# An encoder step on one core: projections emitted tile by tile, with the first norm, the gates, the mixer's first tiles and the tail put in another order

## The chip, the core and the metric
The kernel runs on one core of a Trainium2 chip. The core has a matrix engine (TensorE, in the profile PE, with its weight loads as PEld), a vector engine (VectorE, DVE), a scalar engine (ScalarE, ACT), GpSimd (POOL), and DMA queues, most of them issued by SyncE (SP). Each engine works through its own list of instructions in order and waits for the others on semaphores. The metric is the device time of one execution in microseconds; three timed executions are given by their median.

## What is computed
One layer of a streaming encoder for 576 positions: 512 of a new stream, 64 of a running one with 1024 cached positions. `T` is 576, `D` is 1024; the arrays stand transposed, features on the 128 partitions and positions along a row.

```python
h = rmsnorm(x, g_attn);  z = h @ w_in
q, k, v, f_lin, q_c, c_kv, k_r = split(z)        # 3 x 512 | 8 | 384 | 256 | 32
logf = log_sigmoid(f_lin + b_f)                  # the gates; F = cumsum(logf)
fox = softmax(q k^T / 8 + F[t] - F[s], causal) v              # 8 heads x 64
q_full = rmsnorm(q_c, g_q) @ w_q_up;  c_kv = rmsnorm(c_kv, g_kv)   # the latent norms
mla = softmax((q_lat c_kv^T + rope(q) rope(k_r)^T) / sqrt(96), chunk mask) c_kv w_uv   # 8 heads
x = x + concat(fox, mla) @ w_out
u = rmsnorm(x, g_ffn) @ w_up                      # 2 x 2816 columns
x = x + (silu(conv(gate)) * conv(value)) @ w_down
y = rmsnorm(x, final_norm)
```

Keys, values, gates, latents and the last rows of `u` are outputs as well.

## The kernel before
Every product of full precision is three matmuls: weights and inputs are split into a high and a low part, and low x high, high x high and high x low are added up in PSUM. A weight block of 128x1024 is loaded as `wr`, ScalarE writes its high part and VectorE or GpSimd its low part into `wh` (both have two buffers). PSUM has eight banks in rings: `g` two, `s` three, `t` two, `o` one. A projection tile (`in_tile`) is 48 matmuls over two `g` banks, one bank for each half of the 576 positions; VectorE evacuates them, scaled by `R`, the reciprocal root of the first norm.

The stages, with the times of the profiled execution: to about 20 us `x` is loaded and split and the first key tile, the gates' logits and the rope key are computed beside it; the first norm follows (`sq_sum`, `col_sums`, `rstd`), whose squares ScalarE makes, whose adds go to GpSimd and VectorE by the string `acc0`, and whose sum over partitions is a matmul with `ones`. Projections and attention over 16 heads fill the time to 320 us: FoX in pairs of heads (`fox_gemm(p)`: key, query and value tile of pair p), then MLA. W_out takes until 369 us, the mixer until 784 us, the tail until the end: the last down projection in two halves of the positions (320, then 256), each with the final norm and its output (`L994` on GpSimd, `L996` on VectorE).

What sets the order: five generators (projections, scores and values of the heads, and the same for the running stream) are interleaved by a planner that goes by the costs they yield. The lists thus emitted are then arranged, engine by engine, by a list scheduler of the framework. The projections' generator is `s_gemm`. Its sequence is pair 0 (ahead of it), then pair 1, the five latent tiles `l0` to `l4` (`latent`), pair 2, the two latent norms (`latent_norm`, with their matmuls by `ones`), pair 3, then the keys and queries of MLA, of which the query up-projection is the first to read the normalised and split latents (`xs`). `gates()` is called after all three tiles of pair 1; its result `cf` holds the decay factors that the running stream's scores (L523) read. The mixer (`up_conv`, `gemm`) takes tile after tile; its input is the split and scaled `x2` (`split_scaled`, L267), which is complete only when W_out is.

Of the kernel before, what the change touches and what calls it, by code (L numbers as in the profile page):

```python
# [11 lines left out]
AF = mybir.ActivationFunctionType  # L12
# [43 lines left out]
    "sq0": "a", "acc0": "gggvvv", "sq": "agv", "acc": "gvvv",  # L56
# [9 lines left out]
TPOOL = (0, 1)  # L66

W0 = 6
# [3 lines left out]
def build(nc, tc, io):  # L72
# [177 lines left out]
    def rstd_of(v, y, a, out):  # L250
        S.activation(y, v, AF.Ln)
        S.activation(y, y, AF.Exp, scale=-0.5)
        newton(v, y, a, out)

    def newton(v, y, a, out):
        V.tensor_tensor(a, y, y, op=ALU.mult)
        V.scalar_tensor_tensor(a, a, -0.5, v, op0=ALU.mult, op1=ALU.mult)
        V.scalar_tensor_tensor(out, a, 1.5, y, op0=ALU.add, op1=ALU.mult)

    def rstd(ps, n, out):  # L260
        v, y, a = (raw()[:, :T] for _ in range(3))
        evac(lambda d, p, c: V.tensor_scalar(d, p, 1.0 / n, EPS, op0=ALU.mult, op1=ALU.add), v, ps)
        rstd_of(v, y, a, out)
# [183 lines left out]
    def fox_gemm(p):  # L447
        ps = k0 if p == 0 else in_tile(p)
        k = raw()
        evac(lambda d, p, c: V.tensor_tensor(d, p, R[:, c], op=ALU.mult), k, ps)  # L450
        G.dma_start(io["o_k"][p], k[:, :T])
        ps = in_tile(4 + p)
        q = raw()
        evac(lambda d, p, c: V.scalar_tensor_tensor(d, p, FOX_SCALE, R[:, c], op0=ALU.mult, op1=ALU.mult), q, ps)
        ps = in_tile(8 + p)
# [3 lines left out]
        return q, k, v  # L459
# [96 lines left out]
    fx = {0: fox_gemm(0)}  # L556
    gate = {}

    def gates():
        S.activation(z, z, AF.Identity, bias=bf)  # L560
        mn = raw()[:8, :T]
        V.scalar_tensor_tensor(mn, z, -1.0, z, op0=ALU.mult, op1=ALU.min)
        e = raw()[:8, :T]
        S.activation(e, mn, AF.Exp)
        up = raw()[:8, :T]
# [5 lines left out]
        logf = raw()[:8, :T]  # L571
# [4 lines left out]
        fp = raw()[:8, :T]  # L576
# [166 lines left out]
    def s_gemm():  # L743
        for p in range(1, 4):
            if p >= 2:
                yield ("after", ("stack", 2 * (p - 2) + 1), 0)
            fx[p] = fox_gemm(p)
            if p == 1:
                gates()
            yield ("done", 23.1, ("up", p))  # L750
            if p == 1:
                for a in range(5):
                    latent(a)
                    if a == 2:
                        rope_key()
                    if a == 1:
                        acc_c = sq_sum(craw)
                    if a == 4:
                        acc_q = sq_sum(qcr)
# [143 lines left out]
    def g_tile():  # L903
# [9 lines left out]
        return t[0][:, k * 1152:(k + 1) * 1152].rearrange("p (a b) -> p a b", a=2)  # L913

# [44 lines left out]
    for hf, (o, w) in enumerate(HC):  # L959
# [138 lines left out]
```

## Time and profile before

| | |
|---|---|
| median of three timed executions | 809.66 us (807.43 to 810.17) |
| the profiled execution | 810.69 us, of which the span 808.9 |
| TensorE busy | 772.8 us (96%), 5582 matmuls |
| VectorE, ScalarE, GpSimd busy | 508.5, 340.6, 264.0 us |
| mean granted clock of TensorE | 0.988 of 2.4 GHz |

A granted clock of 1.00 is 2.4 GHz, 0.50 is 1.2 GHz; the clock has these two levels, and a value between them is a mean over a stretch that holds both. Matmuls overlap, so a busy TensorE is not one at its peak; a stretch in which it is idle is one in which it waits.

### The profile page before, as it was taken

How to read it: one execution, taken by the hardware profiler on the slowest of the kernel's cores; microseconds unless marked ns; L12 is line 12 of the kernel's file. 1: busy time of each engine (PE TensorE's matmuls, PEld its weight loads, DVE VectorE, ACT ScalarE, POOL GpSimd, SP SyncE). 2: the span in 40 equal slices, each digit the busy share in tenths (PEclk: the TensorE clock that was granted, in tenths of full speed). 3: DMA queues.
4: the chain of work that ended last, by engine and by line, in shares of the span. 5: the costliest groups of instructions: out<-in, count | busy, mean ns of one | idle time of the engine just before them, and what ended most of it. 6: DMA issues, size and time to landing. Idle time of an engine off the chain costs nothing.

```text
span 808.9 us, 14256 instructions
## 1 busy us (share of the span) xinstructions
PE 772.8 (96%) x5582; PEld 743.3 (92%) x5582; DVE 508.5 (63%) x941; ACT 340.6 (42%) x611; POOL 264.0 (33%) x390
## 2 busy tenths in 40 slices
PE   8898999999899989999999999999999999999994
PEld 8796899897789879999999999999999999999993
DVE  6838554878677763457867524676425667675356
ACT  7224652457667864124443212343113433433231
POOL 5134342336143230223333221433222343332034
PEclk9998999999999999999999999999999999999997
DMA  9373423545563741222222223222232222222313
GB/s 329 111 212 109 109 84 106 145 107 169 129 152 80 185 131 30 80 79 79 72 85 68 79 92 105 79 79 60 79 98 80 103 80 79 79 66 83 105 40 117
DMA packets 33811, 83.98 MB, mean 104 GB/s; under 512 B 6006, under 2 KB 9350, under 8 KB 33744
## 3 DMA queue, kind: packets, MB, share of 16 engines
q1 hardware_dynamic: 31520, 78.55, 32.6%
q0 software_dynamic: 1008, 3.19, 1.1%
q10 hardware_dynamic: 1216, 1.33, 0.5%
q8 instruction: 44, 0.72, 0.4%
q14 instruction: 23, 0.19, 0.1%
HBM read 64.12 MB, written 5.49 MB: 86 GB/s over the span
## 4 chain that ended last, share of the span: by engine, by line
PE 76%; DVE 10%; ACT 5%; DMA 3%; issue 3%; SPq 1%; POOL 1%; DVEq 0%; ACTq 0%; POOLq 0%
PE g L210 31%; PE s L210 19%; PE t L210 12%; PE g L438 3%; PE g L969 1%; DMA mix<-xT 1%; DVE B L382 1%; DVE xs L267 1%; PE s L720 1%; PE t L375 1%; ACT p L326 1%; PE s L969 1%; DMA A<-qr 1%; PE s L522 1%; DVE raw L135 1%
## 5 line engine op out<-in xcount | busy, mean ns | idle before, releaser
L210 PE MATMUL g<-xs,wh 128*128 128x288 f32 (+2 forms) x2028 | 281.1, 295 | 0.3 <-ACT spt L128 0.2
L210 PEld LDWEIGHTS g<-xs,wh 128*128 128x128 f32 x2028 | 271.1, 189 | 1.7 <-ACT spt L128 0.4
L194 ACT ACTIVATE wh<-wr 128x1024 fp32r<-128x1024 f32 (+4 forms) x106 | 99.8, 942 | 204.3 <-PE g L210 88.4
L135 POOL TENSOR_TENSOR wh<-wr,wh 128x1024 fp32r<-128x1024 f32 (+3 forms) x51 | 111.8, 2192 | 216.5 <-ACT wh L194 173.7
L210 PE MATMUL s<-xs,wh 128*128 128x320 f32 (+3 forms) x840 | 121.1, 300 | 2.3 <-DVE xs L267 2.3
L210 PEld LDWEIGHTS s<-xs,wh 128*128 128x128 f32 (+1 forms) x840 | 116.3, 188 | 2.7 <-ACT wh L194 1.8
L210 PE MATMUL t<-xs,wh 128*128 128x256 f32 (+3 forms) x576 | 83.9, 296 | 1.2 <-DVE xs L267 1.2
L210 PEld LDWEIGHTS t<-xs,wh 128*128 128x128 f32 (+1 forms) x576 | 79.1, 188 | 1.6 <-DVE xs L267 1.4
L135 DVE TENSOR_TENSOR wh<-wr,wh 128x1024 fp32r<-128x1024 f32 (+5 forms) x55 | 59.0, 1077 | 13.7 <-ACT wh L194 13.4
L892 POOL COPY KR<-raw 128x2 f32<-128x2 f32 x33 | 14.6, 443 | 94.1 <-DVE raw L890 94.1
L332 POOL TENSOR_SCALAR p<-p,small 128x128 f32<-128x128 f32 (+2 forms) x48 | 27.5, 575 | 50.9 <-DVE small L327 40.8
L896 DVE SCALAR_TENSOR_TENSOR raw<-raw,par 128x578 f32<-128x578 f32 x22 | 33.6, 1526 | 14.0 <-ACT raw L895 14.0
L326 ACT ACTIVATE p<-s,small 128x128 f32<-128x128 f32 (+1 forms) x64 | 33.6, 527 | 12.5 <-DVE small L361 9.2
L920 ACT ACTIVATE raw<-raw 128x578 f32<-128x578 f32 x22 | 15.1, 688 | 54.5 <-DVE raw L897 54.5
L382 DVE TENSOR_TENSOR B<-t,B 128x512 fp32r<-128x512 f32 (+1 forms) x64 | 29.9, 482 | 9.3 <-ACT B L128 9.2
L128 ACT ACTIVATE B<-t 128x512 fp32r<-128x512 f32 (+1 forms) x64 | 26.2, 435 | 17.1 <-PE t L375 16.4
L361 DVE TENSOR_REDUCE small<-s 128x1 f32<-128x128 f32 (+1 forms) x64 | 30.5, 480 | 4.3 <-PE s L359 2.9
L896 DVE SCALAR_TENSOR_TENSOR raw<-pq,par,raw 128x578 f32<-128x578 f32 x11 | 22.7, 2059 | 12.4 <-ACT raw L895 12.4
L375 PE MATMUL t<-ident,p 128*128 128x128 f32 x160 | 29.1, 277 | 1.0 <-DVE B L382 0.5
L890 DVE TENSOR_TENSOR raw<-s,R 128x256 f32<-128x256 f32 x22 | 9.3, 424 | 31.8 <-PE s L210 31.8
L438 PE MATMUL g<-spt,sv 128*128 128x128 f32 x216 | 26.7, 276 | 0.3 <-ACT spt L128 0.2
L438 PEld LDWEIGHTS g<-spt,sv 128*128 128x128 f32 x216 | 25.2, 192 | 1.1 <-ACT spt L128 0.6
(337 smaller groups left out, 1344.1 us busy)
## 6 DMA issues: line engine op xcount, KB each, us to landing
wr<-w_up SPq DMA_DIRECT2D x44, 512.0 KB
wr<-w_dn SPq DMA_DIRECT2D x24, 384.0 KB
wr<-w_in SPq DMA_DIRECT2D x16, 512.0 KB
A<-pq SPq DMA_DIRECT2D x32, 256.0 KB
mix<-xT SPq DMA_DIRECT2D x16, 288.0 KB
wr<-w_out SPq DMA_DIRECT2D x8, 512.0 KB
A<-pq SPq DMA_DIRECT2D x24, 128.0 KB
sk<-k_c SPq DMA_DIRECT2D x4, 512.0 KB
```

Of the source, the lines that this page charges most:

```text
L128: S.activation(dst, src, AF.Copy)
L135: (V if pick(kind) == "v" else G).tensor_tensor(dst, a, b, op=op)
L194: S.activation(hl[:, 0, a:b], r[:, a:b], AF.Copy)
L210: PE.matmul(ps[hf][:M, :w], lhsT=hl[:, wi, kc * M:(kc + 1) * M], rhs=acts[kc][:, xi, o:o + w], start=(kc == 0 and pi == 0), stop=(kc == n ...
L326: S.activation(p, src, AF.Exp, bias=nm, accum_out=sm[:, 0:1])
L332: (G if e == "g" else V).tensor_scalar(p, p, sm[:, 1:2], 1.0, op0=ALU.mult, op1=ALU.mult)
L361: V.reduce_max(nm[:, 0:1], s[:, :W], axis=AX.X, negate=True)
L375: PE.transpose(t[:, P * (i - j):P * (i - j + 1)], st["p"][i][:, P * j:P * (j + 1)], ident)
L382: V.tensor_tensor(ptj[:, 1, off:], t[:, :w], f(ptj[:, 0, off:]), op=ALU.subtract)
L438: PE.matmul(out, lhsT=v[:, j, :], rhs=spt[:, j, :], start=(j == 0), stop=(j == 8))
L896: V.scalar_tensor_tensor(t, u[:, 1:579], par[:, C_CW + 44 + ch:C_CW + 44 + ch + 1], t, op0=ALU.mult, op1=ALU.add)
L969: PE.matmul(ps[:, :w], lhsT=whl[m][:, wi, kc * P:(kc + 1) * P], rhs=g2[kc][:, xi, c], start=(kc == 0 and pi == 0), stop=(kc == n - 1 and p ...
```

## The change
- First norm: all six adds go to VectorE (`acc0`); the copies of the constants `ident`, `bfc` and `sel` wait until the norm is done; `W0` goes from 6 to 5, so that VectorE alone makes the low parts of the first four weight blocks instead of the first five.
- `fox_gemm` yields after each of its three tiles, so that the planner may put attention between them, and `gates()` is called after the key tile of pair 1. Its temporaries come from the ring `mix` instead of `raw`.
- `s_gemm`: the tiles come as pair 1, `l0`, `l1`, pair 2, `l2`, `l3`, `l4`, pair 3, and the two latent norms stand behind pair 3.
- Mixer: its first two tiles (gate 0, value 0) go together, chunk by chunk of the input, and the norm's sum of squares is emitted at the fifth chunk.
- Tail: in the first half GpSimd makes four of the eight outputs, VectorE the others; in the second half GpSimd makes three instead of two, and VectorE reads the scale from PSUM, with a copy by ScalarE for GpSimd.

```diff
-    "sq0": "a", "acc0": "gggvvv", "sq": "agv", "acc": "gvvv",
+    "sq0": "a", "acc0": "v", "sq": "agv", "acc": "gvvv",
-TPOOL = (0, 1)
-
-W0 = 6
+TPOOL = ((0, 1, 2, 3), (0, 1, 2))
+
+W0 = 5
     def consts():
         nc.sync.dma_start(con[:, :N_CON], io["con"])
-        V.tensor_copy(ident, con[:, K_ID:K_ID + P])
-        V.tensor_copy(bfc, con[:, 0:320])
-        V.tensor_copy(sel, con[0:72, K_SEL:K_SEL + 8])
...
-        rstd(col_sums([sq_sum([t[:, :T] for t in x_in[n:n + 4]], "sq0", "acc0") for n in (0, 4)]), D, R)
+        normed = rstd(col_sums([sq_sum([t[:, :T] for t in x_in[n:n + 4]], "sq0", "acc0") for n in (0, 4)]), D, R)
+    with tc.issue_after(normed):
+        V.tensor_copy(ident, con[:, K_ID:K_ID + P])
+        V.tensor_copy(bfc, con[:, 0:320])
+        V.tensor_copy(sel, con[0:72, K_SEL:K_SEL + 8])
...
     def s_gemm():
-        for p in range(1, 4):
-            if p >= 2:
-                yield ("after", ("stack", 2 * (p - 2) + 1), 0)
-            fx[p] = fox_gemm(p)
-            if p == 1:
-                gates()
-            yield ("done", 23.1, ("up", p))
-            if p == 1:
-                for a in range(5):
-                    latent(a)
...
-                    yield ("done", 7.7, ("lat", a))
-            if p == 2:
-                latent_norm(craw, 256, C_GKV, acc_c)
-                latent_norm(qcr, 384, C_GQ, acc_q)
...
+        for what in ("F1", "l0", "l1", "F2", "l2", "l3", "l4", "F3"):
+            n = int(what[1])
+            if what[0] == "F":
+                if n >= 2:
+                    yield ("after", ("stack", 2 * (n - 2) + 1), 0)
+                for j, _ in enumerate(fox_gemm(n)):
+                    if n == 1 and j == 0:
+                        gates()
+                    yield ("done", 6.4, ("part", n))
+                yield ("done", 0, ("up", n))
+            else:
+                latent(n)
...
+        latent_norm(craw, 256, C_GKV, acc["c"])
+        latent_norm(qcr, 384, C_GQ, acc["q"])
...
-    rstd(sumsq(x2), D, R2)
...
+    def up_gemm(chs):
...
+        for kc in range(8):
+            if kc == 4:
+                rstd(sumsq(x2), D, R2)
+            for hl, ps in zip(hls, pss):
+                for hf, (o, w) in enumerate(HB):
+                    for pi, (wi, xi) in enumerate(((0, 1), (0, 0), (1, 0))):
+                        PE.matmul(ps[hf][:, :w], lhsT=hl[:, wi, kc * P:(kc + 1) * P], rhs=x2hl[kc][:, xi, o:o + w],
+                                  start=(kc == 0 and pi == 0), stop=(kc == 7 and pi == 2))
...
+    early.update(up_gemm((0, NCH)))
...
-        newton(v, y, a, r3)
+        if hf:
+
+            newton(v, y, a, pn[:, :w])
+            S.activation(r3, pn[:, :w], AF.Copy)
+            r3, r3g = pn[:, :w], r3
+        else:
+            newton(v, y, a, r3)
+            r3g = r3
...
-                if hf == 0 or m in TPOOL:
+                if m in TPOOL[hf]:
                     G.tensor_scalar(x2[m][:, c], x2[m][:, c], gl, 1.0, op0=ALU.mult, op1=ALU.mult)
-                    G.tensor_tensor(yt[:, j], x2[m][:, c], r3, op=ALU.mult)
+                    G.tensor_tensor(yt[:, j], x2[m][:, c], r3g, op=ALU.mult)
```

The change moves instructions in each engine's list. In the rows below stand the line, the operation, the tile written and the tiles read, the shape, and how often in a row; line numbers are those of each version.

First place: VectorE at the first norm. `raw<-raw` are the adds of squares, `wh` is the low part of a weight block, the four casts into `sl` belong to the gates' selector. Before:

```order
L267 SCALAR_TENSOR_TENSOR xs<-mix,par,xs 128x576 x5
L178 COPY ident<-sp 128x128
L179 CAST bfc<-sp 128x320
L180 COPY sel<-sp 72x8
L499 CAST sl<-sel 72x64 x4
L135 TENSOR_TENSOR raw<-raw 128x576 x3
L135 TENSOR_TENSOR wh<-wr,wh 128x1024
L262 TENSOR_SCALAR raw<-s 128x288 x2
```

and now:

```order
L264 SCALAR_TENSOR_TENSOR xs<-mix,par,xs 128x576 x5
L135 TENSOR_TENSOR raw<-raw 128x576 x6
L135 TENSOR_TENSOR wh<-wr,wh 128x1024
L259 TENSOR_SCALAR raw<-s 128x288 x2
L253 TENSOR_TENSOR raw<-raw 128x576
L254 SCALAR_TENSOR_TENSOR raw<-raw 128x576
L255 SCALAR_TENSOR_TENSOR R<-raw 128x576
L317 COPY ident<-sp 128x128
```

The copies and casts that stood ahead of the adds are behind the norm, and VectorE has six adds instead of three.

Second place: TensorE around the latent norms. `g<-xs,wh` are projections (48 to a tile), `g<-raw,ones` the norms' sums over partitions, `t<-ident,raw` the transposes of a value tile, `s<-...` scores. Before, from the latent tiles and pair 2 (240 matmuls) on:

```order
L210 MATMUL g<-xs,wh 128x288 x240
L230 MATMUL g<-raw,ones 128x288
L341 MATMUL t<-ident,raw 128x128 x2
L522 MATMUL s<-sk,qb 128x384
L523 MATMUL s<-cf,sl 128x384
...
L515 MATMUL s<-A 128x384
L516 MATMUL s<-A 128x384
L359 LDWEIGHTS bfc
L359 MATMUL s<-bfc 128x128
L210 MATMUL g<-xs,wh 128x288 x48
L390 MATMUL o<-B,v 128x256 x3
L210 MATMUL g<-xs,wh 128x288 x96
```

and now, where the 144 matmuls are pair 3, and the last row is the query up-projection's start:

```order
L207 MATMUL g<-xs,wh 128x288 x144
L227 MATMUL g<-raw,ones 128x288
L342 MATMUL t<-ident,raw 128x128 x2
L527 MATMUL s<-sk,qb 128x384
L528 MATMUL s<-cf,sl 128x384
...
L391 MATMUL o<-B,v 128x512
L391 MATMUL o<-B,v 128x384
L376 MATMUL t<-ident,p_2241 128x128
L391 MATMUL o<-B,v 128x384
L391 MATMUL o<-B,v 128x256 x3
L207 MATMUL g<-xs,wh 128x288 x6
```

The 144 matmuls of pair 3 stood behind the norms' sums and stand ahead of them now; between the first sum and the query up-projection there are 67 matmuls.

Third place: VectorE in the tail. `mix<-g,mix` and the like are evacuations of the last down projection, 128x256 those of the second half; `raw<-raw` with 128x256 adds up its squares; `wh<-mix,par,raw` are four outputs of the first half. Before:

```order
L257 SCALAR_TENSOR_TENSOR raw<-raw 128x320
L971 TENSOR_TENSOR mix<-s,mix 128x256
L258 SCALAR_TENSOR_TENSOR raw<-raw 128x320
L978 TENSOR_TENSOR raw<-raw,v 128x256
L971 TENSOR_TENSOR mix<-g,mix 128x256
L978 TENSOR_TENSOR raw<-raw,v 128x256
L978 TENSOR_TENSOR raw<-raw,pq 128x256
L971 TENSOR_TENSOR mix<-t,mix 128x256
L978 TENSOR_TENSOR raw<-raw 128x256 x2
L971 TENSOR_TENSOR mix<-s,mix 128x256
L978 TENSOR_TENSOR raw<-raw 128x256
```

and now:

```order
L254 SCALAR_TENSOR_TENSOR raw<-raw 128x320
L999 TENSOR_TENSOR mix<-s,mix 128x256
L255 SCALAR_TENSOR_TENSOR raw<-raw 128x320
L1006 TENSOR_TENSOR raw<-raw,v 128x256
L1031 SCALAR_TENSOR_TENSOR wh<-mix,par,raw 128x320 x4
L999 TENSOR_TENSOR mix<-g,mix 128x256
L1006 TENSOR_TENSOR raw<-raw,v 128x256
L999 TENSOR_TENSOR mix<-t,mix 128x256
L1006 TENSOR_TENSOR raw<-raw,pq 128x256
L999 TENSOR_TENSOR mix<-s,mix 128x256
L1006 TENSOR_TENSOR raw<-raw 128x256 x2
```

The four outputs stand between the first and the second of the second half's adds.

## Rows read from the trace of the kernel before

**Rows 1.** The page: span, and busy time of TensorE with its share.

```profile
span 808.9 us, 14256 instructions
...
PE 772.8 (96%) x5582; PEld 743.3 (92%) x5582; DVE 508.5 (63%) x941; ACT 340.6 (42%) x611; POOL 264.0 (33%) x390
```

**Rows 2.** Waits of TensorE: line waited for, us in total, times, longest.

```profile
PE s L523 <- DVE cf L590: 3.1, 1, 3.1
PE s L230 <- DVE raw L135: 2.9, 1, 2.9
PE s L210 <- DVE xs L267: 2.3, 2, 1.7
...
PE o L980 <- DVE raw L978: 1.5, 1, 1.5
PE t L210 <- DVE xs L267: 1.2, 1, 1.2
```

**Rows 3.** Busy time by stretch: length, engines with instructions, granted clock, DMA.

```profile
80.00:106.00 26.00, 24.79 (x175) 21.87 (x176) 16.08 (x48) 16.89 (x44) 13.44 (x21) 1.00 0.44 113
106.00:144.00 38.00, 38.00 (x291) 37.91 (x290) 18.12 (x29) 12.10 (x22) 12.32 (x13) 1.00 0.31 94
144.00:156.00 12.00, 11.44 (x68) 8.82 (x67) 9.86 (x25) 6.51 (x17) 2.70 (x6) 1.00 0.64 174
156.00:178.00 22.00, 21.72 (x162) 21.20 (x162) 18.12 (x32) 10.49 (x21) 9.11 (x9) 1.00 0.34 98
178.00:211.00 33.00, 29.66 (x195) 24.25 (x193) 28.83 (x70) 25.33 (x66) 16.20 (x24) 1.00 0.61 163
211.00:230.00 19.00, 17.22 (x113) 15.89 (x113) 11.33 (x29) 11.94 (x29) 4.20 (x8) 1.00 0.54 143
```

**Rows 4.** The same view around the two longest waits.

```profile
24.00:28.00 4.00, 3.56 (x9) 2.68 (x10) 2.26 (x4) 0.00 (x0) 0.00 (x0) 0.57 0.32 101
71.00:80.00 9.00, 7.90 (x32) 5.70 (x32) 6.60 (x21) 4.68 (x14) 5.16 (x6) 0.62 0.42 109
```

**Rows 5.** Timeline of VectorE at the first norm: start, us, instructions.

```profile
18.71 5.67 DVE L135 TENSOR_TENSOR raw<-raw 128x576 f32<-128x576 f32 x3
```

**Rows 6.** Timeline of ScalarE at the first norm.

```profile
13.94 4.69 ACT L220 ACTIVATE raw<-mix 128x576 f32<-128x576 f32 x8
```

**Rows 7.** Timeline of VectorE beside the third pair's projections.

```profile
157.05 1.54 DVE L548 SCALAR_TENSOR_TENSOR mix<-mix,par,raw 128x576 f32<-128x576 f32 x2
...
159.05 0.76 DVE L256 TENSOR_TENSOR raw<-raw 128x576 f32<-128x576 f32 x1
159.85 1.13 DVE L257 SCALAR_TENSOR_TENSOR raw<-raw 128x576 f32<-128x576 f32 x1
161.01 1.62 DVE L258 SCALAR_TENSOR_TENSOR raw<-raw 128x576 f32<-128x576 f32 x1
...
162.92 2.26 DVE L548 SCALAR_TENSOR_TENSOR mix<-mix,par,raw 128x576 f32<-128x576 f32 x3
...
174.28 2.89 DVE L135 TENSOR_TENSOR xs<-mix,xs 128x576 fp32r<-128x576 f32 x4 [0.65 <-ACT xs L552]
...
177.46 1.21 DVE L135 TENSOR_TENSOR xs<-mix,xs 128x576 fp32r<-128x576 f32 x1
```

**Rows 8.** Timeline of VectorE in the tail.

```profile
793.42 1.81 DVE L978 TENSOR_TENSOR raw<-raw 128x256 f32<-128x256 f32 x2
...
796.05 1.02 DVE L978 TENSOR_TENSOR raw<-raw 128x256 f32<-128x256 f32 x1 [0.48 <-ACT raw L976]
...
801.04 1.35 DVE L996 SCALAR_TENSOR_TENSOR v<-mix,par,v 128x256 f32<-128x256 f32 x2
...
803.57 0.87 DVE L996 SCALAR_TENSOR_TENSOR raw<-mix,par,v 128x256 f32<-128x256 f32 x2
```

**Rows 9.** Timeline of GpSimd in the tail.

```profile
790.94 7.69 POOL L994 TENSOR_TENSOR wh<-mix,raw 128x320 f32<-128x320 f32 x8 [0.64 <-DVE raw L258]
801.17 1.79 POOL L994 TENSOR_TENSOR raw<-mix,v 128x256 f32<-128x256 f32 x2 [2.55 <-DVE v L258]
```

More of the change, by code (lines that the diff above doesn't have):

```diff
@@ L252, in rstd_of @@
         S.activation(y, y, AF.Exp, scale=-0.5)
-        newton(v, y, a, out)
+        return newton(v, y, a, out)
     def newton(v, y, a, out):
@@ L257, in newton @@
         V.scalar_tensor_tensor(a, a, -0.5, v, op0=ALU.mult, op1=ALU.mult)
-        V.scalar_tensor_tensor(out, a, 1.5, y, op0=ALU.add, op1=ALU.mult)
+        return V.scalar_tensor_tensor(out, a, 1.5, y, op0=ALU.add, op1=ALU.mult).ins
     def rstd(ps, n, out):
@@ L262, in rstd @@
         evac(lambda d, p, c: V.tensor_scalar(d, p, 1.0 / n, EPS, op0=ALU.mult, op1=ALU.add), v, ps)
-        rstd_of(v, y, a, out)
+        return rstd_of(v, y, a, out)
     def split_scaled(dst, src, g):
@@ L554, in split @@
         return t
-    fx = {0: fox_gemm(0)}
+    fx = {}
+    for _ in fox_gemm(0):
+        pass
     gate = {}
@@ L570, in gates @@
         V.tensor_tensor(up, up, e, op=ALU.add)
-        logf = raw()[:8, :T]
+        logf = mixt()[:8]
         V.scalar_tensor_tensor(logf, z, 0.0, up, op0=ALU.min, op1=ALU.subtract)
@@ L575, in gates @@
         G.memset(zero8, 0.0)
-        fp = raw()[:8, :T]
+        fp = mixt()[:8]
         V.tensor_tensor_scan(fp[:, :NP], logf[:, :NP], zero8[:, :NP], 0.0, op0=ALU.add, op1=ALU.add)
@@ L743, in s_gemm @@
     def s_gemm():
-        for p in range(1, 4):
-            if p >= 2:
-                yield ("after", ("stack", 2 * (p - 2) + 1), 0)
-            fx[p] = fox_gemm(p)
-            if p == 1:
-                gates()
-            yield ("done", 23.1, ("up", p))
-            if p == 1:
-                for a in range(5):
-                    latent(a)
[L754 to L759, printed above, removed]
-                    yield ("done", 7.7, ("lat", a))
-            if p == 2:
-                latent_norm(craw, 256, C_GKV, acc_c)
-                latent_norm(qcr, 384, C_GQ, acc_q)
-                for a in range(2):
-                    G.dma_start(io["o_lat"][a], craw[a])
+        acc = {}
+        for what in ("F1", "l0", "l1", "F2", "l2", "l3", "l4", "F3"):
[10 more added lines that the diff above has]
+                latent(n)
+                if n == 2:
+                    rope_key()
+                if n == 1:
+                    acc["c"] = sq_sum(craw)
+                if n == 4:
+                    acc["q"] = sq_sum(qcr)
+                yield ("done", 6.4, ("lat", n))
+        latent_norm(craw, 256, C_GKV, acc["c"])
+        latent_norm(qcr, 384, C_GQ, acc["q"])
+        for a in range(2):
+            G.dma_start(io["o_lat"][a], craw[a])
         mla_keys()
@@ L877, in build @@
     R2 = sb([P, T], F32, "R", 1)
-    rstd(sumsq(x2), D, R2)
     cs = sb([P, 512], F32, "KR", 1)[:, :176].rearrange("p (a b) -> p a b", b=4)
-    def up_conv(ch):
-        hl = wload(io["w_up"][ch], 1024)
-        ps = psg()
-        gemm(ps, P, hl, x2hl, HB)
+    def up_gemm(chs):
+        hls = [wload(io["w_up"][ch], 1024) for ch in chs]
+        pss = [psg() for _ in chs]
+        for kc in range(8):
[6 more added lines that the diff above has]
+                                  start=(kc == 0 and pi == 0), stop=(kc == 7 and pi == 2))
+        return dict(zip(chs, pss))
+    early = {}
+    def up_conv(ch):
+        ps = early.pop(ch, None)
+        if ps is None:
+            hl = wload(io["w_up"][ch], 1024)
+            ps = psg()
+            gemm(ps, P, hl, x2hl, HB)
         u = raw()
```

11 lines of the change are left out of this document (7 added, 4 removed).

## The prediction

> **What bounds the kernel now.** The first thing read is the share of busy time: TensorE is busy for 772.8 us, 96% of a span of 808.9 us [rows 1]. So a change that takes no matmul away can give back at most the 36 us in which TensorE is idle, plus what its matmuls lose at the half clock. The second view is the list of what TensorE waits for [rows 2]. Its long waits are single events: 3.1 us for `cf`, the decay factors of the gates; 2.9 us for the sum of squares of the first norm; 2.3 and 1.2 us for splits made by VectorE ahead of the mixer; 1.5 us for the last sum in the tail. The third view lays busy time over stretches [rows 3], and tells which engine sets the pace in each. From 106 to 144 us TensorE never waits and VectorE is busy for 18.12 of 38 us: GEMMs, with spare room beside them. From 178 to 211 us it is the other way: VectorE 28.83 of 33 us (87%), TensorE 29.66. That stretch is attention, paced by VectorE. The last view is the granted clock around the two long waits [rows 4]: 0.57 at 24 to 28 us and 0.62 at 71 to 80 us, so TensorE fell to its lower level (1.2 GHz) after each of the two idles of about 3 us.
>
> **First norm: -3.5 us (-4.4 to -1.5).** Before, GpSimd makes three of six adds and VectorE waits its turn behind casts, and its own three take 5.67 us and end at 24.38 us [rows 5]. ScalarE has the last square at 13.94 + 4.69 = 18.63 us [rows 6]. Afterwards six adds stand alone on VectorE. A like sum of two 128x576 tiles takes 0.76 us when nothing is beside it [rows 7], so six take 4.6 us; they can follow the squares, and end near 19.7 us and not before 18.63 + 0.76 = 19.4. That is 4.7 us earlier, more than TensorE's 2.9 us wait, so all of that goes. The half clock behind it cost 3.56 x (1 - 0.57) = 1.5 us [rows 4]. Together 4.4 us. Against it, a value tile is now projected right after the norm, and its evacuation needs the scale `R` from VectorE; if that is late, the next tile of the same two banks waits. I take 0.9 us for that, and 2.9 at the other end.
>
> The moved copies of the constants cost nothing: they are short and the first transposes come only after some 100 matmuls.
>
> **Gates: -3.5 us (-6.1 to -1.0).** The chain of the gates now starts after the key tile of the second pair instead of after its three tiles, and its temporaries leave the `raw` ring. `cf` is wanted by the first scores behind about two more tiles of GEMM, so the 3.1 us wait goes. What the half clock cost is at most 7.90 x (1 - 0.62) = 3.0 us [rows 4], but that stretch is the first softmax, where TensorE waits for exponentials at either clock; I count 0.4 of it. The lower end, 1.0, is a `cf` that is still 2 us late.
>
> **Projections tile by tile, up to the third pair: -1.0 us (-3 to +1).** Heads 1 to 5 are now spread between latent tiles and the second pair, where VectorE had 20 of 38 us free. From 80 to 106 us TensorE had 24.79 of 26 us busy [rows 3]; most of those 1.2 us can go, little more.
>
> **The latent norms: +8 us (2 to 14.6).** This is where the change takes something away. Before, the norms of the latents stand ahead of the third pair, and TensorE runs 21 us of GEMM over their VectorE work. From 156 to 178 us it is busy 21.72 of 22 [rows 3], while VectorE makes the scalings (1.54 and 2.26 us), one set of Newton steps (0.76, 1.13, 1.62) and the five splits (2.89 and 1.21) [rows 7]: 11.4 us, hidden. In the new order the sums of squares come behind the third pair, and TensorE's rows between there and the first use of a split (the query up-projection) are 67 matmuls. They are of the same kinds as the 68 that took 11.44 us of TensorE from 144 to 156 us, beside 9.86 us of VectorE [rows 3]. VectorE then needs 9.86 + 11.4 = 21.3 us where TensorE has 11.4 us: a wait of 9.8 us in all. Part comes back. Some head work moves ahead of the third pair, and the stretch behind, where TensorE now idles 33 - 29.66 = 3.3 us, becomes lighter for VectorE; I take half of these 3.3, 1.7 us, and get +8. The low end lets the later work catch up in all the 19 - 11.33 = 7.7 us that VectorE has free from 211 to 230 us: 9.8 - 7.7 = 2. The high end lets nothing come back, has VectorE at 87% (11.4 / 0.87 = 13.1), and adds one half-clock stretch of the size seen at the first norm, 1.5 us.
>
> **The mixer's first tiles: -0.4 us (-1.2 to 0).** TensorE waits 1.2 us there, at the seventh chunk of the first tile, for the last splits [rows 2], and these VectorE instructions stay as they are. Two tiles are now open at once, but in the new order only four matmuls of the second stand ahead of that chunk. At the 38.00 / 291 = 0.13 us that a matmul takes where TensorE never waits [rows 3], they fill 0.5 us of the wait; I take 0.4.
>
> **Tail: +1.2 us (-0.5 to +2.2).** Before, GpSimd makes eight output tiles of the first half in 7.69 us [rows 9]. Now VectorE makes four of them, and in its queue all four stand ahead of an evacuation and of six of the accumulations that end in the last sum of squares. A pair of such instructions takes 0.87 us where GpSimd is idle and 1.35 where one of the two lies beside GpSimd, so 0.44 and 0.91 us each [rows 8]; these four are 320 wide instead of 256 and lie beside GpSimd's adds at 7.69 / 8 = 0.96 us each: about 1.0 each, 4.0 us. What pays for them is the free time that VectorE has there (0.48 us ahead of its last add and shorter ones, I count 0.8) and the contention that its own adds suffered: 1.81 us for two and 1.02 for a third, 1.5 us over three at 0.44 [rows 8], which a GpSimd with half the work no longer causes. So the last sum comes 4.0 - 0.8 - 1.5 = 1.7 us later. In the second half the scale lies in PSUM, five multiplications at 0.44 take 2.2 us in place of 1.35 x 2 + 0.87 = 3.6 for six, but a copy goes ahead of GpSimd's three (two took 1.79 us [rows 9]), and those end only some 0.5 us before the old end. Together +1.2.
>
> The Trainium skill ("SBUF — State Buffer", section "Who interferes with whom") says that a VectorE instruction with two inputs in SBUF and a GpSimd instruction that reads SBUF shut each other out for a whole instruction, and one with a single SBUF input does not. The 0.91 against 0.44 us fits it. By that rule the second half gains and the first half loses what is counted above, and the sum stays as it is.
>
> **Sum.** -3.5 - 3.5 - 1.0 + 8 - 0.4 + 1.2 = +0.8 us. The profiled execution took 810.69 us, 1.0 above the median of 809.66; on the median the sum is **810.5 us**. A measurement of this kernel can tell about 0.3% (2.4 us) from nothing, so the forecast is no measurable change. Its own range, with two of the terms off by half of their way, is 807 to 814.
>
> **The rivals.** *The give-back is small* (faster). The list of instructions is an order, and TensorE may find more beneath the norms than 67 matmuls: if the third pair's own VectorE work is done early, the norms start with its last matmuls, and later stretches catch up. For it speaks that VectorE has 40% free from 211 to 230 us; against it, that all the splits follow in one queue. With +2 in place of +8 the sum is -5.2, and with 1.5 more of the half clock won back at the gates -6.7: about 803 us. It decides for faster when TensorE's waits between the third pair and the query up-projection stay under 4 us.
>
> *The wait moves and takes the clock with it* (slower). The split is so late that TensorE stands for more than 2.9 us in one piece, as it did twice before a clock drop [rows 2, 4]. Then the latent term is 14.6 in place of 8, the tail with an idle near 3 us its upper 2.2: -3.5 - 3.5 - 1.0 + 14.6 - 0.4 + 2.2 = +8.4, about 818 us. It decides from a wait of some 11 us between the third pair and the query up-projection. For it speaks that the order shows nothing but short attention work there; against it, that this work comes in pieces, each of which ends an idle.
>
> The Trainium skill ("TensorE: Matmul & The Clock Gate", Part 1) says that an idle TensorE is set back to half its clock. The trace agrees at its two idles of 2.9 and 3.1 us. By that rule this rival has its extra 1.5 us, and no more.
>
> *The first two edits do little* (slower by a little). The evacuation that needs `R`, or a softmax that no longer has GEMMs behind it, takes the place of what is removed: -1.5 and -1.0 in place of -3.5 each, sum +5.3, 815 us.
>
> **Chances.** The forecast 0.35, of which 0.33 lie within 0.3% and 0.01 on either side; the small give-back 0.33; the wait with the clock 0.24; the first edits worth little 0.08. So faster 0.34, same 0.33, slower 0.33. The range must reach into the cases on both sides: 799 to 819 us.
>
> **What the changed profile would show.** Right: no wait for sums of squares at 20 to 25 us and a clock of 1.00 from 20 to 80 us; `cf` no longer among the long waits; between the third pair and the query up-projection VectorE over 85% busy and 6 to 10 us of waits of TensorE, for splits or for scores that VectorE evacuates; the last sum in the tail 1 to 2 us later behind its last matmul. Wrong: TensorE over 90% busy in that stretch (then faster), or a granted clock below 1 there (then slower).

## The result, and the profile after

The changed kernel takes 840.26 us (median of four), the kernel before, measured beside it, 808.54: a ratio of 1.0387, 95% interval 1.0365 to 1.041. That is some 31 us slower, beyond the upper end of the forecast's range.

The page of the changed kernel, with its span, TensorE's row and the granted clock in 40 slices:

```profile
span 840.2 us, 14219 instructions
...
PE 787.7 (94%) x5582; PEld 755.0 (90%) x5582; DVE 501.9 (60%) x947; ACT 343.2 (41%) x612; POOL 254.5 (30%) x381
...
PEclk9999999996789999999999999999999999999997
```

TensorE carries out the same 5582 matmuls as before [rows 1], but is busy 787.7 - 772.8 = 14.9 us longer with them, and idle 840.2 - 787.7 = 52.5 us instead of 36.1, 16.4 us more. So half of the loss is idle time of TensorE, and the other half is time in which the same matmuls took longer. That half goes with the clock: the mean granted clock is 0.964 where it was 0.988, and three slices between 189 and 252 us lie at 6 to 8. An estimate from the two means: 840.2 x 0.036 - 808.9 x 0.012 = 20.5 us of full speed are missing, in busy and idle time together, enough for the 14.9.

What TensorE waits for, of the changed kernel (line, us in total, times, longest):

```profile
PE s L728 <- DVE cf L644: 5.7, 1, 5.7
PE o L391 <- DVE B L383: 3.8, 1, 3.8
PE t L376 <- POOL p L333: 3.7, 2, 2.0
PE o L1008 <- DVE raw L1006: 3.4, 1, 3.4
PE s L527 <- ACT p L327: 3.0, 1, 3.0
...
PE g L207 <- DVE raw L461: 2.3, 1, 2.3
```

The long waits of before [rows 2] for the first norm and for the gates' `cf` are gone. New ones stand in their place: 5.7 us for the `cf` of the cached rope keys (L644), 3.8 for a transposed probability tile (`B`) that VectorE evacuates, 3.0 for an exponential. The tail's wait went from 1.5 to 3.4 us.

Busy time by stretch, of the changed kernel, for four stretches in which the clock fell (length, TensorE, weight loads, VectorE, ScalarE, GpSimd, clock, DMA):

```profile
57.00:67.00 10.00, 8.56 (x31) 5.42 (x29) 7.00 (x20) 8.07 (x24) 4.78 (x9) 0.66 0.60 156
99.00:113.00 14.00, 11.33 (x65) 10.14 (x65) 4.82 (x14) 6.10 (x18) 5.95 (x8) 0.76 0.12 37
184.70:213.10 28.40, 17.73 (x77) 11.74 (x75) 24.79 (x55) 16.36 (x40) 11.12 (x13) 0.71 0.34 98
213.10:248.50 35.40, 26.89 (x156) 24.21 (x155) 19.76 (x35) 17.36 (x36) 9.47 (x9) 0.89 0.44 112
```

From 184.7 us (the end of the third pair) to 213.1 (the first matmul of the query up-projection) 28.4 us pass for 77 matmuls, with VectorE busy for 24.79 (87%) and the clock at 0.71. Before, 68 such matmuls took 12 us [rows 3]. The following 35 us run at 0.89. The timeline of TensorE in this stretch, its long waits and the two rows of GEMM at its edges:

```profile
184.73 0.65 PE L227 MATMUL g<-raw,ones 128*128 128x288 f32 x2
...
194.71 0.81 PE L527 MATMUL s<-sk,qb 128*128 128x320 f32 x2 [3.00 <-ACT p L327]
...
212.43 0.79 PE L391 MATMUL o<-B,v 128*128 128x256 f32 x2 [3.81 <-DVE B L383]
213.10 1.81 PE L207 MATMUL g<-xs,wh 128*128 128x288 f32 x6
...
248.47 0.66 PE L728 MATMUL s<-cf,sl 96*128 96x384 f32 x1 [5.69 <-DVE cf L644]
```

and VectorE's timeline, the rows that these waits point to:

```profile
192.37 0.69 DVE L130 CAST sk<-wr 128x1024 fp32r<-128x1024 f32 x1 [2.69 <-DMA wr<-c_T]
...
193.64 0.42 DVE L362 TENSOR_REDUCE small<-s 128x1 f32<-128x256 f32 x1
...
199.42 1.52 DVE L553 SCALAR_TENSOR_TENSOR mix<-mix,par,raw 128x576 f32<-128x576 f32 x2
...
206.84 4.55 DVE L553 SCALAR_TENSOR_TENSOR mix<-mix,par,raw 128x576 f32<-128x576 f32 x3
```

VectorE first stands 2.69 us for the load of the cached latents, with the softmax of two heads queued behind that cast (194.71 in TensorE's rows). Then come the norms, between the heads' rows. The three scalings at 206.84 take 4.55 us, where two and three of them took 1.54 and 2.26 before [rows 7]. One of them alone takes 2.96 us; the median of all five scalings is 0.87. GpSimd was at work beside them, as its timeline shows:

```profile
207.07 2.91 POOL L135 TENSOR_TENSOR xs<-wr,sk 128x1024 fp32r<-128x1024 f32 x1
```

Behind these 4.55 us waits the evacuation of `B`, and TensorE 3.81 us for it. The chain of work that ended last confirms the sequence (start, length, what ran or was waited for):

```profile
187.96 4.39 DMA wr<-c_T
...
206.91 4.47 DVE mix L553 x3
213.22 1.68 PE g L207 x6
...
241.44 4.49 DMA spt<-kr_T
...
247.09 1.29 DVE cf L644
```

It goes from the load of the cached latents over the norms' scalings to the query up-projection, and from there to the load of the rope keys and `cf`.

### The profile page after: what moved, and what is told of

Its sections match the earlier page's. It is cut to its first block, busy times and chain, and to the rows that moved or that the text cites. A ratio compares the mean times of both kernels' runs of the same rounds, so it can differ in the third digit from the quotient of the medians.

```text
span 840.2 us, 14219 instructions
## 1 busy us (share of the span) xinstructions
PE 787.7 (94%) x5582; PEld 755.0 (90%) x5582; DVE 501.9 (60%) x947; ACT 343.2 (41%) x612; POOL 254.5 (30%) x381
## 4 chain that ended last, share of the span: by engine, by line
PE 76%; DVE 8%; DMA 4%; SPq 3%; ACT 3%; issue 3%; POOL 1%; POOLq 0%; ACTq 0%; DVEq 0%
PE g L207 33%; PE s L207 18%; PE t L207 12%; PE g L439 2%; DMA A<-pq 2%; PE t L376 1%; DVE xs L264 1%; PE g L997 1%; SPq L704 1%; PE s L997 1%; PE s L527 1%; PE s L727 1%; ACT wh L191 1%; DVE mix L553 1%; PE o L391 1%
## 5 line engine op out<-in xcount | busy, mean ns | idle before, releaser
L207 PE MATMUL s<-xs,wh 128*128 128x320 f32 (+3 forms) x816 | 117.3, 300 | 1.6 <-DVE xs L264 1.6
L207 PEld LDWEIGHTS s<-xs,wh 128*128 128x128 f32 (+1 forms) x816 | 112.7, 188 | 2.1 <-ACT wh L191 1.2
L207 PE MATMUL t<-xs,wh 128*128 128x320 f32 (+3 forms) x552 | 80.1, 297 | 0.0
L207 PEld LDWEIGHTS t<-xs,wh 128*128 128x128 f32 (+1 forms) x552 | 75.6, 188 | 0.1
L135 DVE TENSOR_TENSOR wh<-wr,wh 128x1024 fp32r<-128x1024 f32 (+5 forms) x55 | 60.8, 1109 | 18.4 <-ACT wh L191 18.1
L918 POOL COPY KR<-raw 128x2 f32<-128x2 f32 x33 | 14.6, 442 | 94.3 <-DVE raw L916 94.3
L376 PE MATMUL t<-ident,p 128*128 128x128 f32 x160 | 32.5, 297 | 6.4 <-POOL p L333 3.7
L376 PEld LDWEIGHTS t<-ident,p 128*128 128x128 f32 x160 | 20.7, 151 | 11.0 <-POOL p L333 5.6
L391 PE MATMUL o<-B,v 128*128 128x256 f32 (+2 forms) x80 | 24.7, 380 | 4.0 <-DVE B L383 3.8
```

The source lines that it names most:

```text
L135: (V if pick(kind) == "v" else G).tensor_tensor(dst, a, b, op=op)
L207: PE.matmul(ps[hf][:M, :w], lhsT=hl[:, wi, kc * M:(kc + 1) * M], rhs=acts[kc][:, xi, o:o + w], start=(kc == 0 and pi == 0), stop=(kc == n ...
L376: PE.transpose(t[:, P * (i - j):P * (i - j + 1)], st["p"][i][:, P * j:P * (j + 1)], ident)
L391: PE.matmul(o[:, q0:], lhsT=vt[:, 2 * j + hh].rearrange("p a d -> p (a d)"), rhs=pts[j][:, a, :], start=(j == 0 and a == 0), stop=(j == 3 ...
```

## The experiments

All ratios are to the kernel before, run on the same chip; 0.001 is 0.8 us. "Busy" and "idle" are TensorE's in the profiled execution.

| run | ratio (95%) | median us | busy | idle | clock |
|---|---|---|---|---|---|
| the changed kernel | 1.0387 (1.0365-1.041) | 840.26 | 787.7 | 52.5 | 0.964 |
| a_normfirst | 1.023 (1.0205-1.0255) | 828.93 | 785.1 | 42.9 | 0.976 |
| a_oldproj | 1.0075 (1.0049-1.0101) | 815.38 | 775.4 | 37.8 | 0.984 |
| a_w6 | 1.039 (1.0357-1.0424) | 840.81 | 785.1 | 51.6 | 0.965 |
| a_normfirst_w6 | 1.0211 (1.0173-1.0248) | 826.53 | 779.5 | 45.2 | 0.978 |
| c_oldseq_parts | 1.0137 (1.0108-1.0166) | 817.71 | 778.3 | 38.7 | 0.977 |
| c_newseq_whole | 1.0133 (1.0117-1.0149) | 818.1 | 775.5 | 40.5 | 0.98 |
| a_oldproj_w6 | 0.9931 (0.9904-0.9957) | 803.59 | 772.1 | 31.4 | 0.988 |
| b_norm | 1.0108 (1.0092-1.0123) | 819.08 | 778.7 | 38.5 | 0.982 |
| b_w0 | 1.0127 (1.0091-1.0163) | 819.24 | 779.4 | 38.8 | 0.982 |
| b_w4 | 1.0006 (0.9989-1.0022) | 809.38 | 774.9 | 34.9 | 0.986 |
| b_accconst | 0.9972 (0.9955-0.9989) | 806.67 | 772.9 | 32.7 | 0.986 |
| b_gates | 0.9901 (0.987-0.9933) | 801.0 | 771.3 | 30.6 | 0.991 |
| b_mix | 0.9988 (0.9965-1.001) | 808.49 | 774.8 | 35.4 | 0.986 |
| b_tail | 0.9999 (0.9982-1.0016) | 810.0 | 773.8 | 35.2 | 0.986 |
| a_kr_own | 1.0298 (1.0258-1.0338) | 834.28 | 784.3 | 45.7 | 0.968 |
| a_cT_act | 1.0352 (1.0308-1.0397) | 838.26 | 789.4 | 48.4 | 0.962 |
| d_gates_mix_acc | 0.9893 (0.9876-0.9911) | 798.02 | 766.4 | 28.4 | 0.994 |
| d_kr_own | 0.9854 (0.9812-0.9896) | 797.64 | 767.2 | 27.6 | 0.991 |

**The projections put back, in whole and in part.** The first theory (N) was that the latent norms behind the third pair cost the time; its rival (P), that the new order of the tiles does. In `a_normfirst` the norms alone go back ahead of the third pair:

```diff
-        for what in ("F1", "l0", "l1", "F2", "l2", "l3", "l4", "F3"):
+        for what in ("F1", "l0", "l1", "F2", "l2", "l3", "l4", "N0", "F3"):
...
+            elif what[0] == "N":
+                latent_norm(craw, 256, C_GKV, acc["c"])
+                latent_norm(qcr, 384, C_GQ, acc["q"])
```

> The changed kernel with one thing put back: the two latent norms are emitted ahead of the third pair's projections instead of behind them; the tiles keep their new order. Theory N (the norms without cover behind the third pair cost the time, with the half clock that follows): most of the 31 us goes, the time is 812 to 822 us, and the granted clock stays at 1.00 where it now falls after the third pair. Theory P (the new order of the tiles as a whole, heads spread between them, costs the time, wherever the norms stand): 825 us or more.

It took 828.93 us: 0.0157 of 809, 12.7 us, go, and 18.6 stay. Each theory had its share, and the larger one belongs to P, whose expectation it met. `a_oldproj` has the old `s_gemm`, with each pair in one piece, in the changed kernel:

```diff
+        for p in range(1, 4):
+            if p >= 2:
+                yield ("after", ("stack", 2 * (p - 2) + 1), 0)
+            for j, _ in enumerate(fox_gemm(p)):
+                if p == 1 and j == 0:
+                    gates()
+            yield ("done", 23.1, ("up", p))
```

> The changed kernel with the old sequence of projections (pair 1, five latent tiles, pair 2, norms, pair 3, each pair as one piece), the gates still called after the key tile of pair 1. Theories N and P both: the loss goes whole, 804 to 812 us, since the projections' sequence holds it. Theory S (the loss comes from the start: first norm, gates, temporaries in the mix ring that delay others): it stays above 825 us.

815.38 us: 25 of the 31 us are the sequence of projections. But it is still slower than before by 0.0075, 6 us, although it holds only edits that I had counted as gains. By elimination these 6 us had to be in the start, the mixer or the tail.

**The single edits, each in the kernel before.** `b_norm` and `b_tail` take the lines of the change's diff for the first norm and for the tail.

> The kernel before with only the first norm's edits (six adds on VectorE, constants behind the norm, W0 of 5). By the prediction's term 3.5 us faster, 805 us; by the rival that the next wait takes its place, within 1.5 us of before.

> The kernel before with only the tail's edits. By the prediction's term 1.2 us slower, 810 us, with the last sum of squares 1.7 us later; by the rival that the second half's gain is the larger, 0.5 us faster.

The tail made no difference that can be measured. The first norm's edits made it 0.0108 slower, 9 us, the opposite of both expectations. They are three edits, and the next runs part them: `b_accconst` holds two, `b_w0` the third.

```diff
-W0 = 6
+W0 = 5
```

> The kernel before with two of the three edits of the first norm (six adds on VectorE, constants behind the norm) and W0 left at 6. Of TensorE's order 12 places differ from before, of VectorE's 9. Theory O (what made all three edits 9 us slower is the order of the attention, which the third edit, W0, changes at some 50 places): these two alone win what the norm's wait held, 803 to 808 us. Theory R (the norm itself, by a late R or the adds on VectorE, costs the 9 us): 815 us or more.

> The kernel before with W0 of 5 alone: one low part of a weight block goes from VectorE to GpSimd, and the order of TensorE's list differs from before at 52 places, VectorE's at 76. Theory O: 815 to 822 us, the loss spread over 60 to 320 us and not at the block itself. Theory R: 808 to 812 us.

Two of the edits win 0.0028, 2.3 us, and `W0` alone loses 0.0127, 10 us. Its loss isn't at the block itself. TensorE's waits in `b_w0` (line, total, times, longest) are those of the attention:

```profile
PE s L523 <- DVE cf L590: 3.7, 1, 3.7
PE g L668 <- ACT raw L645: 3.4, 1, 3.4
...
PE o L390 <- DVE mix L394: 2.1, 1, 2.1
```

The wait of 3.4 us is for an evacuation of the query up-projection, 2.1 for a head's output; neither is long in the kernel before. `W0` decides from which weight block on the low parts go to GpSimd and VectorE by turns. One block less turns the engines of all later blocks of the attention over. `b_w4` tells that from a block that moves alone:

> The kernel before with W0 of 4. The low parts go to GpSimd and VectorE by turns from the block that W0 names, so W0 of 5 turns the engines of all later blocks of the attention over, and W0 of 4 leaves all but one as before (and the order with them: 2 places of TensorE's list differ). Theory T (the turn of the later blocks, and the order that follows from it, cost the 10 us): 807 to 811 us. Theory G (a low part more on GpSimd at the start costs them): 813 us or more.

With `W0` of 4 one block goes to GpSimd and all later ones stay where they were: 1.0006, no difference. The block that moves is the one ahead of the one that `b_w0` moves, a 128x512 part at 10 us, so the run does not move the same block. With that reservation it is the turn of the later blocks, with the order that the framework's list scheduler makes of it, and not a block more on GpSimd at the start. `b_gates` and `b_mix` hold the other two edits:

> The kernel before with the gates' edits alone (called after the key tile of the second pair, temporaries in the mix ring). By the prediction's term 3.5 us faster, 806 us, without the wait for cf and without the half clock from 72 to 79 us; by the rival that the softmax sets the pace there anyway, within 2 us of before; by theory O (28 places of TensorE's order differ) up to 5 us slower with a loss after 100 us.

> The kernel before with the mixer's edit alone (its first two tiles together, chunk by chunk). By the prediction's term 0.4 us faster, which is no difference that can be measured; TensorE's wait for the last splits at 375 us falls from 1.2 to some 0.7 us. By the rival that a whole pair of banks more is held, 1 to 2 us slower.

The mixer's edit makes no difference that can be measured, and the gates' edit wins 0.0099, 8 us (5.4 to 10.5 by its interval), more than its term of 3.5. Busy time in `b_gates` in the stretch of [rows 4]:

```profile
71.00:80.00 9.00, 9.00 (x72) 8.09 (x70) 5.37 (x17) 7.22 (x21) 5.75 (x9) 1.00 0.57 118
```

TensorE has 72 matmuls in these 9 us, at the full clock, where it had 32 before. They are not the same ones: the first head's scores start at 62 us now, with projection matmuls between them, and the next head's fill these 9 us.

**W0 in the changed kernel.** `a_w6`, `a_oldproj_w6` and `a_normfirst_w6` are the changed kernel, `a_oldproj` and `a_normfirst` with `W0 = 6`.

> The changed kernel with W0 put back to 6, all else as changed. If W0 costs here what it cost alone: 840 - 10 = 830 us. If the order of the tiles has turned the blocks over already, so that W0 no longer decides: 836 to 844 us, or another time by the same re-arrangement.

> The changed kernel with the old sequence of projections and W0 of 6: what is left are the six adds on VectorE, the constants behind the norm, the early gates, the mixer's first tiles and the tail. If the single edits add up (2.3, 8 and 0.3 us faster, the tail nothing): 797 to 801 us, faster than both kernels. If the turn of the blocks is not what made W0 slow: 808 us or more.

> The changed kernel with the latent norms ahead of the third pair and W0 of 6. If the two are separate: 829 - 10 = 819 us, and what is left to the old sequence (about 20 us) belongs to the spread of the heads between the tiles.

With the new sequence `W0` decides nothing (1.039 against 1.0387), and only 0.002 with the norms put back (826.53 us, where 819 was expected). With the old sequence it decides 0.0144, 12 us, and without it the remaining edits are faster than before, 0.9931, if not by their sum: 803.59 us where 797 to 801 were expected.

**The two halves of the new sequence.** Between `a_oldproj_w6` and `a_normfirst_w6` lie 23 us, with the norms in the same place. `c_oldseq_parts` has the old order of tiles, handed over tile by tile; `c_newseq_whole` the new order, in whole pairs.

```diff
-        for what in ("F1", "l0", "l1", "F2", "l2", "l3", "l4", "N0", "F3"):
+        for what in ("F1", "l0", "l1", "l2", "l3", "l4", "F2", "N0", "F3"):
```

> The changed kernel with W0 of 6, the norms ahead of the third pair and the five latent tiles together ahead of the second pair, as before; the pairs still go to the planner tile by tile. Against 826.5 us with the new order of the tiles and 803.6 with the old order in whole pairs. If the order of the tiles is what costs: 802 to 807 us. If the tile-by-tile handing over is what costs: 820 us or more.

```diff
-                    yield ("done", 6.4, ("part", n))
-                yield ("done", 0, ("up", n))
+                yield ("done", 23.1, ("up", n))
```

> The changed kernel with W0 of 6, the norms ahead of the third pair, the tiles in the new order, but each pair handed to the planner as one piece. If the order of the tiles is what costs: 820 to 828 us. If the tile-by-tile handing over is what costs: 802 to 810 us.

Neither expectation holds: each half alone costs 0.0206 and 0.0202 against `a_oldproj_w6`, 17 and 16 us, and both together 0.028. One more thing differs in each of them: the costs that the planner is given, 6.4 for a latent tile where `a_oldproj_w6` has 7.7, and in `c_oldseq_parts` 3 x 6.4 for a pair instead of 23.1. No run parts them from the order and the handing over.

The two halves lose in different stretches. Busy time up to 120 us and from there to 260 us, of `a_oldproj_w6`, `c_oldseq_parts` (with two shorter stretches) and `c_newseq_whole`:

```profile
20.00:120.00 100.00, 96.79 (x682) 90.92 (x682) 64.07 (x142) 45.17 (x95) 36.92 (x46) 0.97 0.46 133
120.00:260.00 140.00, 132.42 (x885) 118.37 (x884) 102.31 (x229) 83.12 (x201) 52.33 (x69) 0.99 0.48 129
```

```profile
52.00:68.00 16.00, 13.80 (x55) 9.33 (x54) 9.83 (x29) 9.80 (x27) 7.20 (x10) 0.68 0.64 152
98.00:112.00 14.00, 10.44 (x60) 9.58 (x60) 7.63 (x16) 6.86 (x17) 8.27 (x9) 0.76 0.14 44
20.00:120.00 100.00, 93.83 (x624) 85.56 (x623) 61.19 (x138) 43.36 (x92) 36.70 (x46) 0.91 0.43 126
120.00:260.00 140.00, 127.75 (x865) 115.74 (x864) 94.64 (x209) 73.25 (x174) 47.15 (x63) 0.98 0.45 121
```

```profile
20.00:120.00 100.00, 97.47 (x704) 90.98 (x701) 65.16 (x145) 45.01 (x94) 37.20 (x45) 1.00 0.51 143
120.00:260.00 140.00, 122.42 (x800) 110.48 (x799) 94.53 (x204) 73.22 (x175) 46.34 (x64) 0.94 0.39 109
```

The handing over by tiles loses time before 120 us already, where the clock is 0.91 instead of 0.97, and it brings the two stretches of the changed kernel with a fallen clock: 0.68 and 0.76 here, 0.66 and 0.76 there. In both kernels the first of them holds scores and transposes of heads in a row, with no projection matmul between. The order of the tiles loses nothing before 120 us and 10 us of TensorE's busy time behind it. TensorE's waits in `c_oldseq_parts`:

```profile
PE s L728 <- ACT cf L645: 5.1, 1, 5.1
PE g L429 <- POOL sp L333: 3.5, 1, 3.5
```

and in `c_newseq_whole`:

```profile
PE s L728 <- ACT cf L645: 3.5, 1, 3.5
...
PE t L376 <- DVE v L346: 3.2, 1, 3.2
PE g L227 <- DVE raw L135: 2.6, 1, 2.6
PE g L207 <- DVE raw L259: 2.3, 1, 2.3
```

In the second kernel the norms' sums (L227) and what follows them (L259) wait, 2.6 and 2.3 us. With pair 2 ahead of the last three latent tiles nothing stands between these tiles and the norms, so the squares, their adds and the evacuations are no longer covered. These two waits are 4.9 of the 9.1 us that TensorE idles more than in `a_oldproj_w6`. In the old order pair 2's 144 matmuls stood there. Both kernels wait longer for the rope keys' `cf` (L645, 5.1 and 3.5 us) than `a_oldproj_w6` (1.9). What delays that in the first, and how much of its 17 us is the order of the later heads, I have not parted further.

**The chain behind the third pair.** Two runs take a link out of it in the changed kernel: `a_kr_own` moves the block that loads the rope keys ahead of the split of the latents and gives it another buffer, `a_cT_act` has the cast at 192.37 us made by ScalarE.

```diff
-        krc = sb([32, 1152], F32, "spt", 1)
+        krc = f(xst().rearrange("p a b -> p (a b)"))[:32]
```

> The changed kernel with the load of the cached rope keys in a buffer of its own kind (a free xs tile) and emitted ahead of the cached latents' split, so that SyncE issues it some 50 us earlier. If the 5.7 us wait for cf behind it is a wait of its own: it goes, with the half clock that follows, 831 to 835 us. If VectorE and ScalarE set that time anyway: the next wait takes its place, 838 us or more.

```diff
-    "kva": "v", "spl": "v", "cTh": "vaav", "cTl": "gggv", "qlh": "av",
+    "kva": "v", "spl": "v", "cTh": "aaav", "cTl": "gggv", "qlh": "av",
```

> The changed kernel with the first high part of the cached latents made by ScalarE instead of VectorE, so that VectorE doesn't stand 2.7 us for their load with the softmax of two heads behind it. If that wait starts the chain: TensorE's 3.0 us wait goes, and 835 us or less. If the norms' VectorE work sets the pace from the third pair to the query up-projection: no more than 2 us, 838 us or more.

In `a_kr_own` the 5.7 us wait is gone, and 0.0089 with it, 7 us, as expected; those ahead of it stand:

```profile
PE o L391 <- DVE B L383: 3.8, 1, 3.8
...
PE s L527 <- ACT p L327: 3.0, 1, 3.0
```

It was a wait of its own. In `a_cT_act` a longer wait for an exponential took the first one's place, and the one for `B` became 2.8 us:

```profile
PE s L520 <- ACT p L327: 6.6, 5, 3.4
PE s L728 <- ACT cf L645: 5.7, 1, 5.7
...
PE o L391 <- DVE B L383: 2.8, 1, 2.8
```

Its ratio, 1.0352, and that of the changed kernel have intervals that overlap: 3 us or nothing. That fits the reading that the VectorE work of the norms sets the pace there, but does not show it alone: ScalarE got the cast, and the new wait is for ScalarE.

**A faster version.** `d_gates_mix_acc` is the kernel before with the gates', the mixer's and the adds' edits (`acc0`), without `W0`, the moved constants, the sequence or the tail; `d_kr_own` has the early rope keys as well.

> The kernel before with the early gates, the mixer's first tiles together and the six adds on VectorE; old sequence, old tail, constants and W0 as before. If the single gains add up: 801 - 0.3 - 2 = 799 us. If the earlier norm only moves the first softmax's wait forward (the kernel with all edits but the sequence took 803.6): 801 to 804 us.

> The kernel with early gates, mixer and adds (798 us) and the rope keys' early load. The wait of 1.9 us for cf goes: 796 to 797 us; or no difference, if the re-arranged order (25 places of TensorE's list) takes it back.

798.02 us, 0.9893, is faster than both kernels and near the 799 expected. The interval overlaps that of the gates' edit alone (0.9901), so that the other two edits add to it is not shown. TensorE is idle for 28.4 us instead of 36.1. Its busy time from 20 to 106 us:

```profile
20.00:106.00 86.00, 85.91 (x629) 81.00 (x629) 60.95 (x131) 43.37 (x92) 35.71 (x45) 1.00 0.50 149
```

85.91 of 86 us. `d_kr_own` has the same time (797.64; the intervals overlap).

## Why the prediction was wrong

*The step that failed* is the term for the projections tile by tile up to the third pair: -1.0 us (-3 to +1). The new order of the tiles and their handing over, with the planner's costs that go with them, cost +0.028, 23 us (`a_normfirst_w6` against `a_oldproj_w6`). The step argued from VectorE's free time in the GEMM stretch: 20 of 38 us, so heads may be put there. That is true and did not decide. What it left out is what the same GEMMs had covered. For the order of the tiles the runs show it in part: pair 2's GEMM behind the last latent tiles had covered the squares and their adds, and without it their sums wait (2.6 and 2.3 us in `c_newseq_whole`). For the handing over tile by tile `c_oldseq_parts` shows where the time goes: heads stand in a row without projections between them, TensorE idles (3.5 us in one piece for a scaling by GpSimd), and the clock is 0.68 and 0.76. Why the planner and the scheduler then leave the heads without projections, by the tiles or by the costs, stays open.

*The latent norms*: the mechanism was right, and the size lies near the range's high end. The prediction had +8 (2 to 14.6); putting them back gains 0.0157 and 0.0179 (with `W0` of 5 and of 6), 12.7 and 14.5 us. VectorE's 21.3 us came out as 24.79 in a stretch of 28.4. The wait was forecast well: TensorE idles 28.4 - 17.73 = 10.7 us there, where the term had 9.8. What it had wrong is TensorE's own time, 17.73 us instead of 11.4: 77 matmuls in the trace where the order listed 67, and a clock of 0.71. The half of the following stretch's idle time that I let come back did not come back: that stretch got the wait for `cf`, 5.7 us, 7 us of the time by `a_kr_own`; with the norms put back TensorE doesn't wait for it. The rival with the clock described the stretch (a wait over 2.9 us in one piece, the clock falling behind it), but priced the clock at 1.5 us.

*The first norm*: the adds ended at 20.0 us (predicted 19.7), and the sums of squares no longer wait:

```profile
15.13 4.88 DVE L135 TENSOR_TENSOR raw<-raw 128x576 f32<-128x576 f32 x6 [0.33 <-ACT raw L217]
```

```profile
21.69 1.13 PE L227 MATMUL s<-raw,ones 128*128 128x288 f32 x4
...
40.23 0.51 PE L207 MATMUL g<-xs,wh 128*128 128x288 f32 x2 [2.33 <-DVE raw L461]
```

The wait in TensorE's rows, 2.33 us at 40.23, is the value tile's evacuation (L461), for which the term had 0.9 to 2.9. By themselves the adds and the moved constants win 2.3 us, near the -3.5. But `W0` was read as one block of work that moves. In the order of before it is worth +10 us, and the term held nothing for it. In the new sequence it is worth nothing, so this oversight is not what made the changed kernel slow.

*The gates*: right in kind, too small: -8 us instead of -3.5; the interval of 5.4 to 10.5 holds the term's end of -6.1. The half clock of that stretch was counted at 0.4 us because the softmax would wait anyway. It did not: the first scores now run from 62 us on, between projection matmuls, and TensorE is busy for all of the 9 us, at a clock of 1.00 instead of 0.62.

*The mixer's first tiles*: -0.4 predicted, 0.9988 measured; the two agree within the measurement. TensorE's wait there fell from 1.2 to 0.9 us in `b_mix`, where 0.7 was expected.

*The tail*: +1.2 predicted, 0.9999 (0.9982 to 1.0016) measured, which neither confirms nor excludes it. Its two parts are to be seen in `b_tail`, VectorE's timeline and then TensorE's:

```profile
790.37 4.46 DVE L1003 SCALAR_TENSOR_TENSOR wh<-mix,par,raw 128x320 f32<-128x320 f32 x4
...
802.01 0.87 DVE L1003 SCALAR_TENSOR_TENSOR v<-mix,par,o 128x256 f32<-128x256 f32 x2 [0.45 <-ACT v L989]
```

```profile
794.16 0.51 PE L969 MATMUL s<-sv,xs 128*128 128x256 f32 x3
798.08 0.70 PE L980 MATMUL o<-raw,ones 128*128 128x256 f32 x2 [3.41 <-DVE raw L978]
```

The four outputs took 4.46 us (predicted 4.0). TensorE's wait for the last sum is 3.41 us where it was 1.54, 1.9 later (predicted 1.7). From that sum to the end of the span 809.0 - 798.08 = 10.9 us pass, where it was 808.9 - 797.1 = 11.8. The outputs with the scale from PSUM take 0.44 us each (0.87 for two), the first pair while GpSimd makes its three from 802.10 us on. The Trainium skill ("SBUF — State Buffer", section "Who interferes with whom") says that a VectorE instruction with at most one input in SBUF, outside its two-port modes, does not contend with GpSimd; these rows agree.

Together: the single edits outside the sequence and `W0` come to -2.3 - 8 - 1 + 0 = -11 us, and in one kernel (`a_oldproj_w6`) to -5.6. From there the sequence adds 23 for the tiles and 14.5 for the norms, steps of one chain of runs that ends at `a_w6`, 32 us. Why the single edits win only half of their sum together stays open; `d_gates_mix_acc`, which leaves out the moved constants and the tail, wins 8.7.

Of the signs named, these came true: no wait for the first norm's sums, the gates' `cf` gone from the long waits, VectorE at 87% between the third pair and the query up-projection, and the tail's last sum 1.9 us later. The clock of 1.00 from 20 to 80 us did not: it was 0.66 from 57 to 67 us. And the sign for slower, a clock below 1 behind the third pair, was there, at 0.71.

## What to carry to other kernels

A long GEMM is worth not only its own time: ask of each stretch of it what finishes underneath, on every engine and queue, and price a move by what then stands uncovered, at both ends. Where an alternation of engines or a list scheduler decides the order, a one-word edit at the start can re-arrange everything behind it. So compare the two orders as a whole, and time each edit by itself before they go together. A wait of TensorE costs its length and, where the clock falls behind it, much of that again.

## What the runs showed of the hardware

The clock was the surprise. The same matmuls took TensorE 14.9 us more, nearly half of the loss, where I had counted 1.5 at most. It fell not only behind single idles of about 3 us, as before, but also in the stretch from 57 us on, where the longest idle was 1.44 us among short attention matmuls, and in the one from 99 us on, with idles of 0.44, 1.77 and 0.46 us. The Trainium skill ("TensorE: Matmul & The Clock Gate", Part 1) says that an idle TensorE is set back to half its clock; the rows agree in kind, and here it happened without one long idle. An idle of about that size did not always do it: in the kernel before, the 1.8 us wait for the rope keys' `cf` at 220 us lies in a stretch with a clock of 1.00 [rows 3]. By and large the granted clock goes with the time over the runs: 0.994 at 798 us, 0.988 at 810, 0.976 at 829, 0.964 at 840.

A second point is VectorE beside GpSimd. One scaling of 128x576 took 2.96 us beside a GpSimd instruction of 2.91 us in the changed kernel. In `a_normfirst`, with no such instruction beside them, all five take 0.81 to 0.82 us.
